# A hybrid mixer block on one core: dilated scores of two heads in one run of 64-row matmuls, and a new order of the down products

## The chip, the cores and the metric

The kernel runs on one core of a Trainium2 chip. The time is that of the device in microseconds (us). The kernel before took 1464.97 us in the median of three runs (1462.9 to 1469.22).

## The reference

A transformer block with a sequence of 1024 and a width of 1024. Four mixers of width 256 (dilated attention, retention, gated linear attention, a state space layer) share one input projection. Then come an output product, a layer norm, an attention to a memory of 256 rows, a second norm, a SwiGLU network of width 2816, and a third norm:

```python
proj = x @ w_in
y = concat(dilated(dq, dk, dv), retention(...), gla(...), s5(...)) @ w_mix_out
x = layer_norm(ALPHA * x + y);  x = layer_norm(ALPHA * x + memory(x, mem))
x = layer_norm(ALPHA * x + (silu(x @ w_gate) * (x @ w_up)) @ w_down)
# dilated: 4 heads of 64; three branches (window 128, 512, 2048; step 1, 4, 16), joined by their softmax sums
s = q @ k.T * 64 ** -0.5 + alibi;  p = exp(s - max);  o = sum over branches of p @ v, over the sum of p
```

## The kernel before, in words

All data is float32. Where one pass is too coarse, a number is split into a high part (rounded to fp32r) and the rest (fp32r too), and a product is high by high, high by low and low by high: `mm3`, three matmuls into one PSUM bank.

**The order.** Every matmul and transpose goes through `mm` or `tp`, and `pin` ties each to the one before: TensorE runs exactly the order in which the code is written. VectorE (DVE), ScalarE (ACT), GpSimd (POOL) and the DMA queue on SyncE (SP) get their order from the framework's scheduler. The mixers are generators. A `yield t` in one lets `weave` (line 106) put projection work between its parts: about t us of it, in steps that the projection declares (0.65 us for three matmuls of 512 columns, tile `fm`); what was given too much is taken off the next yield.

**Dilated attention** (`dilated(f)`, line 962, once for each pair of heads). The three branches become one softmax, with a table `Z` that holds position terms, masks and the log of how many branches see a key. For query block i (128 queries) n = 128 (i+1) keys count. `scores(j)`, j = 2i + h, handles one head: for each 512 keys one matmul with 128 contraction rows (64 rows of the head's high q above 64 rows of its low q, against the high k stacked twice) and one with 64 rows (high q by low k). Then DVE adds `Z` and takes the maximum in one instruction (line 988), negates it (line 990), and ACT takes the exponential in place (line 991). `turn(j)` transposes the result on TensorE into the PSUM tile that held the scores and copies it to `dpT`; `values(i)` multiplies by v, the two heads side by side in 64 columns each. The layout of the stacked operands is made as the projection is evicted: `ev_q` (line 885) with two casts and two subtractions of 64 rows for each half, `ev_k` (line 896) with four casts and two subtractions.

**The last stage** (`ffn`, line 741). The network runs as a Strassen-like scheme of 7 products. Each of the products of the down projection sums over 11 pairs of operands that lie in device memory; `down_raw` loads a pair (two transfers of 256 KB into one of three buffers `wraw`), `versions` splits it on ACT (line 147) and DVE (line 148) into one of four pairs `whi`, `wlo`. `product` runs 12 matmuls for each pair into four PSUM banks and evicts these at its end. The seventh product (A22 by T4) is loaded and split early, a pair at a time, by `keep`, into tiles of its own; the tuple `ahead` says at which steps of a product. `low` evicts and normalises the rows of the first four tiles, `high` those of the last four.

Of the kernel before, what the change touches and what calls it, by code (L numbers as in the profile page):

```python
# [18 lines left out]
P = 128  # L19
# [16 lines left out]
class Kernel:  # L36
# [704 lines left out]
    def ffn(self, out):  # L741
# [25 lines left out]
        for t in range(NT):  # L767
            self.X.append(self.big("X"))
            nc.sync.dma_start(self.X[t], self.xdr[t])
        g, b = self.bcast_row("ln_ff_g"), self.bcast_row("ln_ff_b")  # L770
        self.vs = self.down_stream([("A11", "B11"), ("S2", "T2"), ("A12", "B21"), ("S1", "T1"), ("S4", "B22"),
# [113 lines left out]
    def ev_q(self, name):  # L885
        t = [None, None]
        self.t[name] = t

        def evac(hf, ps):
            if hf == 0:  # L890
                t[:] = [self.big("q", F32R) for _ in range(2)]
            sl, r = slice(hf * 512, (hf + 1) * 512), [slice(0, 64), slice(64, 128)]
            self.split_all([[t[h][r[h], sl], t[h][r[1 - h], sl], ps[r[h]]] for h in range(2)])
        return evac

    def ev_k(self, name):
        res = [None, None, None]
        self.t[name] = res

        def evac(hf, ps):  # L900
            if hf == 0:
                for h in range(3):
                    res[h] = self.big("k", F32R)
            sl = slice(hf * 512, (hf + 1) * 512)
            r = [slice(0, 64), slice(64, 128)]
            for h in range(2):
                self.nc.scalar.copy(out=res[h][r[1 - h], sl], in_=ps[r[h]])
            self.split_all([[res[h][r[h], sl], res[2][r[h], sl], ps[r[h]]] for h in range(2)])
        return evac
# [52 lines left out]
    def dilated(self, f):  # L962
# [8 lines left out]
        pb, tb = [self.big("dp") for _ in range(2)], [self.big("dpT") for _ in range(3)]  # L971
# [3 lines left out]
        def scores(j):  # L975
            i, h = j // 2, j % 2
            n = (i + 1) * P
            if h == 0:
                l[i] = self.small("dl", [P, 2])
            s = st[j] = self.two("ds")  # L980
# [5 lines left out]
            p = pb[j % 2]  # L986
            m = self.small("dm", [P, 1])
            nc.vector.tensor_tensor_reduce(out=p[:, :n], in0=s[:, :n], in1=Z[h][:, 1024 - n:],
                                           scale=0.125, scalar=-3e38, op0=ALU.add, op1=ALU.max, accum_out=m)
            nc.vector.tensor_scalar(out=m, in0=m, scalar1=-1.0, scalar2=None, op0=ALU.mult)  # L990
            nc.scalar.activation(out=p[:, :n], in_=p[:, :n], func=AF.Exp, bias=m, scale=1.0,
                                 accum_out=l[i][:, h:h + 1])

        def turn(j):
            i = j // 2
            p, pT, t = pb[j % 2], tb[j % 3], st.pop(j)
            for b in range(i + 1):
                self.tp(t[:, b * P:(b + 1) * P], p[:, b * P:(b + 1) * P])
            n = (i + 1) * P
            for c0 in range(0, n, 512):  # L1000
                c1 = min(n, c0 + 512)
                self.copy(pT[:, c0:c1], t[:, c0:c1])

        def values(i):
            if i % 4 == 0:
                o[i // 4], rl[i // 4] = self.tr("do"), self.half("drl")
            for b in range(i + 1):
                for h in range(2):
                    hh = 2 * f + h
                    self.mm(o[i // 4][64 * h:64 * h + 64, i % 4, :], v[b][:, hh * 64:(hh + 1) * 64],  # L1010
                            tb[(2 * i + h) % 3][:, b * P:(b + 1) * P], start=b == 0, stop=b == i, tile_position=(0, 64 * h))
# [673 lines left out]
    def items_all(self):  # L1685
# [4 lines left out]
        for f in range(2):  # L1690
            self.item(f"q{f}", self.fill_fm([self.ev_q(f"q{f}")]), fm(2 * f))
            self.item(f"k{f}", self.fill_fm([self.ev_k(f"k{f}")]), fm(2 * f + 1))
# [124 lines left out]
```

## Time and profile before

| | |
|---|---|
| median of the runs | 1464.97 us |
| profiled execution | 1460.22 us, span 1458.4 us |
| TensorE busy | 1420.3 us, 97% of the span |
| VectorE, ScalarE, GpSimd busy | 935.3, 527.3, 329.5 us |
| granted TensorE clock | 0.996 |
| DMA | 193.61 MB, mean 133 GB/s |

The span counts from the first to the last instruction that was profiled. Matmuls are pipelined: one starts before the one ahead of it has ended, so that the time of a run of matmuls is read from start to start, and the share of busy time counts stretches in which the array takes in less than it could. The idle time in front of an instruction is put down to what released it.

### The profile page before, as it was taken

What the parts mean: (1) busy time and instruction counts of PE and PEld (TensorE: products, weight loads), DVE (VectorE), ACT (ScalarE), POOL (GpSimd) and SP (SyncE); (2) the same over time, 40 slices, a digit from 0 to 9 for tenths busy, and PEclk for the clock granted to TensorE, in tenths of its full rate; (3) what the DMA queues carried; (4) which work ended last, traced back from release to release, by engine and by line L of the source; (5) the groups of instructions that cost most, each with busy time, mean ns of one, the idle gap of its engine ahead of it and who ended that gap; (6) DMA issues with size and microseconds to landing.
All of it is one profiled execution on the core that took longest, in us unless ns stands there. A gap on an engine that the chain in (4) does not pass through costs nothing.

```text
span 1458.4 us, 20809 instructions
## 1 busy us (share of the span) xinstructions
PE 1420.3 (97%) x7754; PEld 1160.0 (80%) x7754; DVE 935.3 (64%) x1640; ACT 527.3 (36%) x834; POOL 329.5 (23%) x592
## 2 busy tenths in 40 slices
PE   8998999999999999999999999999999999999987
PEld 6876787788788788888888877788888888888776
DVE  7877545485567379558557987666655555545586
ACT  4224523342245133334344622222222222345452
POOL 2000000010000000000000256767666665000013
PEclk9999999999999999999999999999999999999999
DMA  7431020100438202214312435445545459666752
GB/s 255 131 119 71 30 73 30 43 31 2 151 102 303 88 29 87 73 44 154 107 45 89 156 124 168 164 166 168 183 150 169 170 174 339 200 189 216 230 189 101
DMA packets 76404, 193.61 MB, mean 133 GB/s; under 512 B 9088, under 2 KB 9872, under 8 KB 76304
## 3 DMA queue, kind: packets, MB, share of 16 engines
q1 hardware_dynamic: 74576, 189.15, 39.2%
q10 hardware_dynamic: 1728, 3.15, 0.7%
q8 instruction: 61, 1.00, 0.3%
q14 instruction: 39, 0.32, 0.1%
HBM read 147.04 MB, written 45.22 MB: 132 GB/s over the span
## 4 chain that ended last, share of the span: by engine, by line
PE 78%; DVE 7%; DMA 6%; issue 3%; POOL 3%; ACT 2%; SPq 1%; DVEq 0%; ACTq 0%; POOLq 0%
PE ga L71 9%; PE gc L71 8%; PE fm L71 8%; PE q L71 6%; PE gb L71 6%; PE wo L71 6%; PE mx L71 5%; PE da L71 5%; DVE wlo L148 2%; PE dn L71 2%; PE ds L71 2%; DMA wraw<-tT 2%; PE dr L71 2%; PE p L71 2%; PE gv L71 2%
## 5 line engine op out<-in xcount | busy, mean ns | idle before, releaser
L148 DVE TENSOR_TENSOR wlo<-wraw,whi 128x1024 fp32r<-128x1024 f32 (+3 forms) x180 | 228.3, 1270 | 118.1 <-ACT whi L147 117.2
L147 ACT CAST whi<-wraw 128x1024 fp32r<-128x1024 f32 (+3 forms) x180 | 186.5, 1038 | 309.9 <-PE mx L71 42.1
L71 PE MATMUL ga<-xv,whi 128*128 128x512 f32 x528 | 163.5, 390 | 4.7 <-DVE gq L693 3.5
L71 PEld LDWEIGHTS ga<-xv,whi 128*128 128x128 f32 x528 | 98.7, 188 | 27.8 <-issue 6.9
L71 PE MATMUL gc<-xv,whi 128*128 128x512 f32 x352 | 109.0, 391 | 1.4 <-ACT ge L678 1.4
L71 PE MATMUL gb<-xv,whi 128*128 128x512 f32 x352 | 108.3, 389 | 0.0
L71 PE MATMUL ga<-xv,wlo 128*128 128x512 f32 x264 | 102.7, 389 | 0.0
L71 PE MATMUL fm<-xh,whi 128*128 128x512 f32 x208 | 85.7, 412 | 0.0
L71 PE MATMUL wo<-whi,oT 128*128 128x512 f32 x256 | 82.1, 394 | 0.0
L71 PE MATMUL fm<-xh,wlo 128*128 128x512 f32 x208 | 81.5, 392 | 0.0
L71 PE MATMUL fm<-xl,whi 128*128 128x512 f32 x208 | 81.3, 391 | 0.0
L71 PE MATMUL mx<-whi,yT 128*128 128x512 f32 x256 | 80.6, 392 | 0.6 <-DVE X L352 0.6
L71 PEld LDWEIGHTS gc<-xv,whi 128*128 128x128 f32 x352 | 65.6, 188 | 15.9 <-ACT ge L678 2.3
L71 PEld LDWEIGHTS gb<-xv,whi 128*128 128x128 f32 x352 | 66.1, 188 | 13.7
L71 PE MATMUL gc<-xv,wlo 128*128 128x512 f32 x176 | 68.5, 389 | 0.0
L71 PE MATMUL gb<-xv,wlo 128*128 128x512 f32 x176 | 68.5, 389 | 0.0
L260 POOL TENSOR_TENSOR X<-X,ln_ff_b 128x1024 f32<-128x1024 f32 x7 | 17.7, 2547 | 196.2 <-ACT X L259 196.2
L71 PEld LDWEIGHTS ga<-xv,wlo 128*128 128x128 f32 x264 | 49.6, 188 | 10.3
L71 PEld LDWEIGHTS mx<-whi,yT 128*128 128x128 f32 x256 | 48.1, 188 | 11.3 <-DVE X L352 1.0
L71 PEld LDWEIGHTS wo<-whi,oT 128*128 128x128 f32 x256 | 48.1, 188 | 9.7
L71 PE MATMUL da<-wlo,whi 128*128 128x512 f32 x132 | 51.7, 392 | 3.9 <-DVE wlo L148 3.9
L71 PE MATMUL dr<-whi 128*128 128x512 f32 x132 | 51.6, 391 | 1.7 <-DVE X L781 1.7
(501 smaller groups left out, 3345.8 us busy)
## 6 DMA issues: line engine op xcount, KB each, us to landing
wraw<-in_w_gu SPq DMA_DIRECT2D x28, 512.0 KB, 4.1
gr<-in_w_gu SPq DMA_DIRECT2D x22, 512.0 KB, 4.5
dw<-in_w_down SPq DMA_DIRECT2D x22, 512.0 KB, 3.9
tT<-dw SPq DMA_DIRECT2D x44, 256.0 KB, 2.0
wraw<-hS SPq DMA_DIRECT2D x44, 256.0 KB, 2.9
wraw<-tT SPq DMA_DIRECT2D x44, 256.0 KB, 3.4
wraw<-hA SPq DMA_DIRECT2D x33, 256.0 KB, 2.8
wraw<-in_w_down SPq DMA_DIRECT2D x33, 256.0 KB, 3.0
```

The costliest lines, as they stand in the source:

```text
L71: return self.pin(self.nc.tensor.matmul(*a, **k))
L147: return (self.nc.scalar.copy(out=hi, in_=src), self.nc.vector.tensor_tensor(out=lo, in0=src, in1=hi.bitcast(F32), op=ALU.subtract))
L148: self.nc.vector.tensor_tensor(out=lo, in0=src, in1=hi.bitcast(F32), op=ALU.subtract))
L260: nc.gpsimd.tensor_tensor(out=x, in0=x, in1=b, op=ALU.add)
```

## The change

The scores of both heads are computed by `scores(i)`, in matmuls of 64 contraction rows only, alternating between the heads (rows 0 to 63 and 64 to 127, two PSUM tiles). The stacked operands go, and with them two tiles and the extra casts: `ev_hl` makes one high and one low tile of all 128 rows. The loop turns both heads one behind the other, and the yields are new. In the last stage the products stand in another order, the keeps sit in the third to fifth product, and the loads of x are written in two places.

```diff
-        for t in range(NT):
-            self.X.append(self.big("X"))
-            nc.sync.dma_start(self.X[t], self.xdr[t])
+        def more_x(ts):
+            for t in ts:
+                self.X.append(self.big("X"))
+                nc.sync.dma_start(self.X[t], self.xdr[t])
+
+        more_x(range(4))
...
-        self.vs = self.down_stream([("A11", "B11"), ("S2", "T2"), ("A12", "B21"), ("S1", "T1"), ("S4", "B22"),
+        self.vs = self.down_stream([("A12", "B21"), ("A11", "B11"), ("S2", "T2"), ("S1", "T1"), ("S4", "B22"),
                                     ("S3", "T3")])
...
-        ac = [self.bank("da") for _ in range(4)]
-        product(ac, True, lambda j, ps: add(X[j], hs[0], ps, ALPHA))
-        product(ac, False, lambda j, ps: add(X[j], hs[1], ps, ALPHA))
+        r, ac = [[self.bank(n) for _ in range(4)] for n in ("dr", "da")]
+        product(r, True, lambda j, ps: add(X[j], hs[0], ps, ALPHA))
+        product(ac, True, lambda j, ps: self.residual(X[j], hs[0], 0, ps, 1.0))
+        more_x(range(4, 8))
+        product(ac, False, lambda j, ps: add(X[j], hs[1], ps, ALPHA), (1, 4, 7, 10))
         r = [self.bank("dr") for _ in range(4)]
-        product(r, True, lambda j, ps: self.residual(X[j], hs[0], 0, ps, 1.0))
-        r = [self.bank("dr") for _ in range(4)]
-        product(r, True, lambda j, ps: add(X[4 + j], hs[1], ps, ALPHA), (2, 5, 8))
-        product(r, False, low, (1, 4, 7, 10))
-        product(ac, False, high, (2, 5, 8, 10))
+        product(r, True, lambda j, ps: add(X[4 + j], hs[1], ps, ALPHA), (1, 4, 7, 10))
+        product(r, False, low, (2, 5, 8))
+        product(ac, False, high)
...
+    def ev_hl(self, name):
+        t = []
         self.t[name] = t
 
         def evac(hf, ps):
             if hf == 0:
+                t.extend(self.big(name[0], F32R) for _ in range(2))
             sl = slice(hf * 512, (hf + 1) * 512)
+            self.split_all([[t[0][:, sl], t[1][:, sl], ps]])
         return evac
...
+        def scores(i):
+            n, qt = (i + 1) * P, slice(i * P, (i + 1) * P)
+            l[i] = self.small("dl", [P, 2])
+            for h in range(2):
+                st[2 * i + h] = self.two("ds")
             for c0 in range(0, n, 512):
                 c1 = min(n, c0 + 512)
-                r, qt = slice(64 * h, 64 * h + 64), slice(i * P, (i + 1) * P)
-                self.mm(s[:, c0:c1], q[h][:, qt], k[h][:, c0:c1], start=True, stop=False)
-                self.mm(s[:, c0:c1], q[h][r, qt], k[2][r, c0:c1], start=False, stop=True)
...
+                for a, b in ((0, 0), (1, 0), (0, 1)):
+                    for h in range(2):
+                        r = slice(64 * h, 64 * h + 64)
+                        self.mm(st[2 * i + h][:, c0:c1], q[a][r, qt], k[b][r, c0:c1], start=a + b == 0, stop=b == 1)
+            for h in range(2):
+                s, p = st[2 * i + h], pb[h]
+                m = self.small("dm", [P, 1])
...
         scores(0)
-        scores(1)
         yield 4.45
-        for j in range(17):
-            if j < 16:
-                turn(j)
-            if j and j % 2 == 0:
-                values(j // 2 - 1)
-            if j == 8 or j == 16:
-                back(j // 8 - 1)
-            yield 1.9
-            if j + 2 < 16:
-                scores(j + 2)
+        for i in range(8):
+            turn(2 * i)
+            turn(2 * i + 1)
+            yield 1.3 + 0.1 * i
+            values(i)
+            if i % 4 == 3:
+                back(i // 4)
+            if i < 7:
+                scores(i + 1)
+                yield 1.8 + 0.25 * i
```

Three places show how the instructions move. First TensorE, the scores of query block 4 of the first pair of heads (640 keys). Before, head 0 alone; `ds` is the PSUM tile of a head's scores, `k` and `q` the stacked operands, the transposes (`ident`) are of the block ahead, and `fm` is projection work:

```order
L71 MATMUL fm215_1772<-xl27_314,whi139_1174 128x512
L71 MATMUL fm215_1772<-xh38_360,wlo140_1175 128x512
L71 MATMUL ds219_1806<-k163_1491,q147_1250 128x512
L71 MATMUL ds219_1806<-k165_1495,q147_1250 128x512
L71 MATMUL ds219_1806<-k163_1491,q147_1250 128x128
L71 MATMUL ds219_1806<-k165_1495,q147_1250 128x128
L74 MATMUL ds216_1776<-ident23_267,dp176_1568 128x128 x4
L71 MATMUL fm215_1772<-xh41_390,whi139_1174 128x512
```

The same block now, both heads (`ds218`, `ds219`), `k163` and `q147` the high, `k164` and `q148` the low tiles:

```order
L71 MATMUL ds218_1805<-k163_1487,q147_1250 128x512
L71 MATMUL ds219_1806<-k163_1487,q147_1250 128x512
L71 MATMUL ds218_1805<-k163_1487,q148_1252 128x512
L71 MATMUL ds219_1806<-k163_1487,q148_1252 128x512
L71 MATMUL ds218_1805<-k164_1489,q147_1250 128x512
L71 MATMUL ds219_1806<-k164_1489,q147_1250 128x512
L71 MATMUL ds218_1805<-k163_1487,q147_1250 128x128
L71 MATMUL ds219_1806<-k163_1487,q147_1250 128x128
L71 MATMUL ds218_1805<-k163_1487,q148_1252 128x128
L71 MATMUL ds219_1806<-k163_1487,q148_1252 128x128
L71 MATMUL ds218_1805<-k164_1489,q147_1250 128x128
L71 MATMUL ds219_1806<-k164_1489,q147_1250 128x128
```

Two times four matmuls in two places, of 128 and 64 rows in turn, have become twelve of 64 rows in one run.

Second DVE, query block 7 of the first pair (1024 keys): line 988 (now 977) adds the table and takes the maximum (`dm`, its second row reads that out), line 990 (now 979) negates it for the exponential. Before:

```order
L988 ISA dp_1566,dm_2026<-ds_2021,Z_1560 128x1024
L988 ISA dm_2026 128x1
L184 COPY dpT_1572<-ds_1979 128x512
L990 TENSOR_SCALAR dm_2026<-dm_2026 128x1
L184 COPY gk_1969<-fm_1972 128x512
L988 ISA dp_1568,dm_2054<-ds_2049,Z_1563 128x1024
L988 ISA dm_2054 128x1
L148 TENSOR_TENSOR wlo_2087<-wraw_2084,whi_2086 128x1024
L990 TENSOR_SCALAR dm_2054<-dm_2054 128x1
```

And now:

```order
L977 ISA dp_1552,dm_2056<-ds_2042,Z_1546 128x1024
L977 ISA dm_2056 128x1
L977 ISA dp_1554,dm_2060<-ds_2043,Z_1549 128x1024
L977 ISA dm_2060 128x1
L184 COPY gk_1982<-fm_1985 128x512
L979 TENSOR_SCALAR dm_2056<-dm_2056 128x1
L148 TENSOR_TENSOR wlo_2071<-wraw_2068,whi_2070 128x1024
L979 TENSOR_SCALAR dm_2060<-dm_2060 128x1
```

The negation of the first head, on which its exponential waits, now stands behind the maximum of the second head; a copy or a weight split stands between, as before.

Third SP, the queue where the down products begin: `X` are the loads of x, `wraw` those of the first product's operands, `tT` and `hA` stores of the products before, `ln_ff` the last norm's vectors. Before (four loads of X stand further ahead):

```order
L769 DMA X_10756<-xdr_87 128x1024
L769 DMA X_10759<-xdr_88 128x1024
L609 DMA tT_210<-dw_10730 128x512
L712 DMA hA_161<-h_10482 128x512
L769 DMA X_10762<-xdr_89 128x1024
L609 DMA tT_209<-dw_10732 128x512
L769 DMA X_10765<-xdr_90 128x1024
L217 DMA ln_ff_g_10768<-in_ln_ff_g 128x1024
L609 DMA tT_211<-dw_10732 128x512
L217 DMA ln_ff_b_10771<-in_ln_ff_b 128x1024
L733 DMA wraw_10792<-in_w_down 128x512
L730 DMA wraw_10811<-hA_112 128x512
```

Now (again with four loads of X further ahead):

```order
L217 DMA ln_ff_g_10772<-in_ln_ff_g 128x1024
L217 DMA ln_ff_b_10775<-in_ln_ff_b 128x1024
L609 DMA tT_210<-dw_10746 128x512
L712 DMA hA_161<-h_10498 128x512
L733 DMA wraw_10800<-in_w_down 128x512
L609 DMA tT_209<-dw_10748 128x512
L770 DMA X_11230<-xdr_87 128x1024
L770 DMA X_11233<-xdr_88 128x1024
L609 DMA tT_211<-dw_10748 128x512
L770 DMA X_11236<-xdr_89 128x1024
L770 DMA X_11239<-xdr_90 128x1024
L730 DMA wraw_10819<-hA_113 128x512
```

The later four loads of X are written behind two products, but the scheduler has put them in front of the first product's next pair; what moved is the order among X, the vectors and half a pair.

## Rows read from the trace of the kernel before

**Rows 1.** The page, busy time, share of the span and instructions of each engine:

```profile
PE 1420.3 (97%) x7754; PEld 1160.0 (80%) x7754; DVE 935.3 (64%) x1640; ACT 527.3 (36%) x834; POOL 329.5 (23%) x592
```

**Rows 2.** The page, chain that ended last, by engine:

```profile
PE 78%; DVE 7%; DMA 6%; issue 3%; POOL 3%; ACT 2%; SPq 1%; DVEq 0%; ACTq 0%; POOLq 0%
```

**Rows 3.** Busy time by stretch: both dilated halves, the last product's begin:

```profile
core 0: us, PE busy (x) PEld busy (x) DVE busy (x) ACT busy (x) POOL busy (x), PEclk, DMA share, GB/s
121.00:200.00 79.00, 77.88 (x399) 54.28 (x399) 43.63 (x103) 37.95 (x73) 1.28 (x14) 1.00 0.14 47
200.00:290.00 90.00, 90.00 (x640) 71.01 (x636) 41.50 (x116) 28.35 (x58) 1.77 (x20) 1.00 0.13 42
...
1380.00:1420.00 40.00, 36.11 (x157) 28.95 (x156) 33.04 (x85) 21.87 (x27) 2.76 (x2) 1.00 0.62 193
```

**Rows 4.** Groups of 121 to 290 us, scores: count, busy us, mean ns, idle before:

```profile
L71 PE MATMUL ds<-k,q 128*128 128x512 f32 (+3 forms) x96 | 35.0, 412 | 1.1 <-ACT s5t L1605 1.0
...
L71 PEld LDWEIGHTS ds<-k,q 128*128 128x128 f32 x96 | 17.8, 185 | 18.5 <-issue 14.4 <-ACT s5t L1605 1.2 <-DVE dpT L184 0.5
```

**Rows 5.** Timeline of TensorE, query blocks 3 and 4: start, length, count:

```profile
160.09 0.88 PE L71 MATMUL do<-dpT,dv 128*64 128x128 f32 x12
160.89 0.50 PE L71 MATMUL fm<-xh,whi 128*128 128x512 f32 x1
161.23 0.39 PE L71 MATMUL fm<-xl,whi 128*128 128x512 f32 x1
161.46 0.40 PE L71 MATMUL fm<-xh,wlo 128*128 128x512 f32 x1
...
163.07 1.33 PE L71 MATMUL ds<-k,q 128*128 128x512 f32 x4
164.32 0.66 PE L74 MATMUL ds<-ident,dp 128*128 128x128 f32 x4
```

**Rows 6.** Timeline of TensorE and its weight loads, one score block of retention:

```profile
408.70 0.52 PEld L71 LDWEIGHTS rs<-rq,rk 64*128 64x128 f32 x8 [0.35 <-issue]
408.70 0.72 PE L71 MATMUL rs<-rq,rk 64*128 64x128 f32 x8
...
409.35 0.39 PE L71 MATMUL kt<-memh,whi 128*128 128x256 f32 x1
```

**Rows 7.** Instructions of tile dp: ns least, median, most:

```profile
L988 DVE CUSTOM_DVE_ANT_0 dp<-ds,Z x32: 291/758/1224, 133.9 to 274.3; 128x128 f32<-128x128 f32 x4, 128x256 f32<-128x256 f32 x4, 128x384 f32<-128x384 f32 x4, 128x512 f32<-128x512 f32 x4
L991 ACT ACTIVATE dp<-dp,dm x32: 393/779/1155, 134.6 to 276.6; 128x128 f32<-128x128 f32 x4, 128x256 f32<-128x256 f32 x4, 128x384 f32<-128x384 f32 x4, 128x512 f32<-128x512 f32 x4
```

**Rows 8.** Groups of 121 to 290 us on VectorE and ScalarE:

```profile
L148 DVE TENSOR_TENSOR wlo<-wraw,whi 128x1024 fp32r<-128x1024 f32 x8 | 9.8, 1219 | 0.9 <-ACT whi L147 0.9
...
L154 DVE TENSOR_TENSOR k<-fm,k 64x512 fp32r<-64x512 f32 x8 | 5.5, 687 | 1.6 <-ACT k L152 1.5
L990 DVE TENSOR_SCALAR dm<-dm 128x1 f32<-128x1 f32 x32 | 4.8, 149 | 0.5
L907 ACT CAST k<-fm 64x512 fp32r<-64x512 f32 x8 | 4.6, 581 | 3.5 <-PE fm L71 3.4
...
L988 DVE DVE_READ_ACCUMULATOR2_ANT dm<- 128x1 f32 x32 | 2.7, 83 | 0.0
```

**Rows 9.** The page, down products, first matmuls of the steps: idle before, releaser:

```profile
L71 PE MATMUL da<-wlo,whi 128*128 128x512 f32 x132 | 51.7, 392 | 3.9 <-DVE wlo L148 3.9
L71 PE MATMUL dr<-whi 128*128 128x512 f32 x132 | 51.6, 391 | 1.7 <-DVE X L781 1.7
```

**Rows 10.** Chain of 1331 to 1339 us: one load of the stream, start, us:

```profile
1331.68 4.40 DMA wraw<-tT
...
1336.15 1.06 ACT dv L147
...
1337.30 1.24 DVE dv L148
1338.55 0.32 SPq L730
```

More of the change, by code (lines that the diff above doesn't have):

```diff
@@ L883, in proj_first @@
         self.nc.sync.dma_start(self.ydr[8], t)
-    def ev_q(self, name):
-        t = [None, None]
+    def ev_hl(self, name):
+        t = []
         self.t[name] = t
@@ L890, in evac @@
             if hf == 0:
[L891 to L903, printed above, removed]
+                t.extend(self.big(name[0], F32R) for _ in range(2))
             sl = slice(hf * 512, (hf + 1) * 512)
[L905 to L908, printed above, removed]
+            self.split_all([[t[0][:, sl], t[1][:, sl], ps]])
         return evac
@@ L970, in dilated @@
             Z.append(z)
-        pb, tb = [self.big("dp") for _ in range(2)], [self.big("dpT") for _ in range(3)]
+        pb, tb = [self.big("dp") for _ in range(2)], [self.big("dpT") for _ in range(2)]
         y = self.big("ya")
         st, l, o, rl = {}, {}, {}, {}
[L975 to L980, printed above, removed]
+        def scores(i):
[3 more added lines that the diff above has]
+                st[2 * i + h] = self.two("ds")
@@ L981, in scores @@
             for c0 in range(0, n, 512):
                 c1 = min(n, c0 + 512)
-                r, qt = slice(64 * h, 64 * h + 64), slice(i * P, (i + 1) * P)
-                self.mm(s[:, c0:c1], q[h][:, qt], k[h][:, c0:c1], start=True, stop=False)
-                self.mm(s[:, c0:c1], q[h][r, qt], k[2][r, c0:c1], start=False, stop=True)
[L986 to L989, printed above, removed]
@@ L990, in scores @@
-            nc.vector.tensor_scalar(out=m, in0=m, scalar1=-1.0, scalar2=None, op0=ALU.mult)
-            nc.scalar.activation(out=p[:, :n], in_=p[:, :n], func=AF.Exp, bias=m, scale=1.0,
-                                 accum_out=l[i][:, h:h + 1])
+                for a, b in ((0, 0), (1, 0), (0, 1)):
+                    for h in range(2):
+                        r = slice(64 * h, 64 * h + 64)
+                        self.mm(st[2 * i + h][:, c0:c1], q[a][r, qt], k[b][r, c0:c1], start=a + b == 0, stop=b == 1)
@@ new lines, in scores @@
+            for h in range(2):
+                s, p = st[2 * i + h], pb[h]
+                m = self.small("dm", [P, 1])
+                nc.vector.tensor_tensor_reduce(out=p[:, :n], in0=s[:, :n], in1=Z[h][:, 1024 - n:],
+                                               scale=0.125, scalar=-3e38, op0=ALU.add, op1=ALU.max, accum_out=m)
+                nc.vector.tensor_scalar(out=m, in0=m, scalar1=-1.0, scalar2=None, op0=ALU.mult)
+                nc.scalar.activation(out=p[:, :n], in_=p[:, :n], func=AF.Exp, bias=m, scale=1.0,
+                                     accum_out=l[i][:, h:h + 1])
@@ L994, in turn @@
         def turn(j):
             i = j // 2
-            p, pT, t = pb[j % 2], tb[j % 3], st.pop(j)
+            p, pT, t = pb[j % 2], tb[j % 2], st.pop(j)
             for b in range(i + 1):
@@ L1010, in values @@
                     self.mm(o[i // 4][64 * h:64 * h + 64, i % 4, :], v[b][:, hh * 64:(hh + 1) * 64],
-                            tb[(2 * i + h) % 3][:, b * P:(b + 1) * P], start=b == 0, stop=b == i, tile_position=(0, 64 * h))
+                            tb[h][:, b * P:(b + 1) * P], start=b == 0, stop=b == i, tile_position=(0, 64 * h))
             nc.vector.reciprocal(out=l[i], in_=l[i])
@@ L1690, in items_all @@
         for f in range(2):
-            self.item(f"q{f}", self.fill_fm([self.ev_q(f"q{f}")]), fm(2 * f))
-            self.item(f"k{f}", self.fill_fm([self.ev_k(f"k{f}")]), fm(2 * f + 1))
+            self.item(f"q{f}", self.fill_fm([self.ev_hl(f"q{f}")]), fm(2 * f))
+            self.item(f"k{f}", self.fill_fm([self.ev_hl(f"k{f}")]), fm(2 * f + 1))
         self.item("gk", self.fill_fm([self.ev_fm("gk", 0)]), fm(12))
```

## Prediction

> **What bounds the kernel.** I read the page's busy times first: TensorE has work in flight for 97% of the span [rows 1]; then the chain that ended last: 78% of it is TensorE [rows 2]. So time is won only where TensorE needs less of it or waits less, and the next view is the busy time by stretch. The two dilated halves lie between 121 and 290 us, and there TensorE is busy for 77.9 of 79 us and all of 90 us [rows 3]; its one wait at the scores is 1.0 us at the start [rows 4]. VectorE and ScalarE are half idle there. What the change saves on TensorE in these halves is therefore saved in full, and any wait it brings in is paid in full, since TensorE keeps the written order. At the end of the program the down products wait: 3.9 us for a weight split and 1.7 us for an eviction [rows 9], 5.6 us together.
>
> **Scores, what goes.** 96 matmuls keep TensorE busy for 35.0 us [rows 4]. A block's end overlaps the next start: the block at 163.07 lasts 1.33 us, the transposes begin at 164.32, 0.08 us before its end [rows 5]. For some 30 blocks that is 2.4 us, so the scores take 32.6 us from start to start. The block of 1.25 us has four matmuls, two of 512 and two of 128 columns. A plain 512-column matmul follows the one ahead by 0.23 us (161.23 to 161.46) [rows 5], so the four would take some 0.7 us; the rest is the change between 128 and 64 rows, four times in the block.
>
> **Scores, what comes.** 144 matmuls of 64 rows, that is 72 steps of two heads. Whether the two of a step run together is not shown by the old scores, which never put the two halves of the rows side by side. The nearest row is retention's score block, where heads alternate between the same two halves of rows: eight matmuls of 128 columns last 0.72 us, and the next product starts 0.65 us after the first of them [rows 6]. Four 128-row transposes of 128 columns take 0.66 us [rows 5], so twice as many half-row matmuls take the same: they go two by two. That block gives four steps of about 0.11 us and 0.2 us for changing into and out of 64 rows. A projection matmul behind such a change takes 0.34 us instead of 0.23 (160.89 to 161.23 to 161.46) [rows 5], 0.1 us more.
>
> The blocks of 128 to 1024 keys make, for both halves, 36 steps of 512 columns and 12 each of 128, 256 and 384. By 0.23 us for 512, 0.11 for 128, and 0.12 and 0.17 for those between (interpolated), that is 8.3 + 1.3 + 1.4 + 2.0 = 13.0 us. Sixteen runs with 0.3 us of changes add 5.0: 18.0 us. Twelve value runs that went back to projection work now lead into the scores, and their 0.1 us each goes too, 1.3 us with rounding. So 32.6 + 1.3 - 18.0 = 16 us are won. Bounds: 21 us if changes cost nothing, 3 us if the two of a step do not overlap at all (13 us more).
>
> A row of the trace decides on the weight loads too: in retention's block eight loads lie within 0.52 us, beside matmuls that last until 0.72 us [rows 6], so loads for a half of the rows do not wait until that half's matmul is through. The Trainium skill says otherwise (page "TensorE: Matmul & The Clock Gate", section "The mechanism"): a weight load overlaps matmuls in flight only when its row group differs. By that rule the second and third pair of weights of each run would be exposed, and the score runs would come out near the unpaired bound; the trace speaks against it.
>
> **Scores, the wait that comes in.** Before, the next head's scores, other transposes and projection work always lay between a head's scores and its transposes. Now both heads are scored together and only a yield of 1.8 to 3.3 us stands before both are turned. The maximum takes 0.29 us for 128 keys up to 1.22 for 1024, the exponential 0.39 to 1.16 [rows 7], a negation 0.15 and the read-out 0.08 [rows 8]. VectorE's new order runs both maxima before the first negation. So the first head is ready 2 maxima + 1 exponential + 0.4 us (read-outs, negation, hand-over) after the scores, the second one exponential and 0.1 us later. Weave's carrying over gives 3, 3, 3, 4, 5, 5, 5 groups of three projection matmuls (0.69 us each) for blocks 1 to 7: 2.1, 2.1, 2.1, 2.8, 3.5, 3.5, 3.5 us. Block 3 (512 keys): ready after 2 x 0.69 + 0.73 + 0.4 = 2.5 us, 0.4 late; the second head after 3.3, when 0.44 us of transposes have moved TensorE to 2.9: 0.4 late again. Block 7: 4.0 and 5.3 us against 3.5 and 4.9: 0.9 late. All seven: 0, 0.4, 0.8, 0.5, 0.1, 0.5, 0.9 = 3.2 us, twice 6.4. A copy or a weight split (1.22 us [rows 8]) in front of a negation adds to a few of them: I take 7 us. Below, the bound is 0 (projection work of gv covers more than I count); above, 6.4 + 14 x 1.22 = 23 us, a split in front of every turn. Behind each waiting transpose stand the values, the next scores and the projection work: all of TensorE.
>
> **Edits that cost nothing.** The evictions lose 16 casts of 0.58 us on ScalarE and 8 subtractions of 0.69 us on VectorE [rows 8]. They lie beside a full TensorE; without that cover they would be worth some 9 us. Two tiles fewer, and 1.2 us less projection work asked for in each half, move work to later parts and change no sum. The loads of X stay in front of the first product by SP's order; were they to push its operands back, it would be one load, 4.4 us [rows 10].
>
> **Down products.** A load takes 4.40 us, its cast 1.06, its subtraction 1.24, the next issue 0.32 [rows 10]: 7.0 us in three buffers, 2.34 us a load. TensorE takes a pair every 12 x 0.23 = 2.75 us. A product without keeps gains 4.5 us on TensorE, one with four keeps (15 loads, 35.1 us against 30.3) loses 4.8. Both versions put 11 keeps into three neighbouring products: 25.7 us of loads against 13.5 us of spare time, 12.2 us behind. Waits of 5.6 us show, so what is loaded and split ahead covered 6.6. The new order moves this forward. At the fourth product's end eight keeps have gone through instead of three: 8 x 2.34 - 22 x 0.41 = 9.7 us behind, 3.1 more than that cover, beside the 1.7 us of that eviction, which sits behind splits in VectorE's queue. The fifth loses about 1 more. The last product is freed of four keeps, but the norms still fill VectorE (33 of 40 us [rows 3]), so of 3.9 us there I keep 1.7. Sum 7.5 against 5.6: 2 us lost. Bounds: 5.6 us won, 6.6 lost.
>
> **Sum.** -16 + 7 + 2 = -7 us on the profiled execution's 1460.22 us: 1453. The median of the runs is 1464.97, 4.8 above it, so I predict 1458 for the median; all times below are on that footing.
>
> **Rivals.** (A) The new waits stay under 3 us and the keeps save 2: -16 + 3 - 2 = -15, 1450. For it: VectorE is busy for only 44 of 79 us [rows 3]. Against: the order of the negations.
> (B) The steps do not overlap, in the streams or in the weight loads: 13 us more, -3 + 7 + 2 = +6, 1471. For it: the mean load of the scores' weights is 0.185 us [rows 4], and 64-row matmuls of this type and 512 columns side by side are in no row. Against: [rows 6]. The Trainium skill's rule above would bring it about by the loads.
> (C) Slower: the transposes wait for VectorE at every turn, because a split or copy of the projection sits between maximum and negation. Place: line 979. Price: 23 us of waits, -16 + 23 + 2 = +9, 1474. It decides from 14 us of waits on; slower beyond 0.5% from 21. For it: such a split stands there at block 7, and ScalarE already depends on these negations. Against: the splits are only 8 in both halves [rows 8].
> (D) The stream loses its full 6.6 us: -16 + 7 + 7 = -2, 1463. For it: three products with keeps follow each other as before. The part of the change that should spread the loads of X does not do it by SP's order, in every case.
>
> **Chances.** Forecast 0.45 (its own range 1452 to 1464), A 0.20, B 0.12, C 0.12, D 0.11. What a measurement of this kernel can tell from no change is 0.5%, 7.3 us. Faster than that: A, and half of the forecast, 0.43. Slower: most of C and a third of B, 0.15. Within: 0.42. The range 1446 to 1474 leaves out the best end of A and the far end of C.
>
> **What would show it.** Right: the scores' busy time falls from 35.0 to about 20 us, two `ds` matmuls start within some 0.02 us of each other, and the transposes `ds<-ident,dp` show 5 to 10 us of idle time behind the exponential (line 980 then). B would show score blocks of four or six matmuls that follow each other by 0.23 us. C would show over 14 us at the transposes. In the down products I expect the wait at the fourth product's end to grow to 4 or 5 us and those of the last to shrink. The prediction is wrong if the score runs take over 25 us, if the transposes wait for nothing, or if the down products' waits vanish.

## The result, and the profile after

In the first comparison the changed kernel takes 1444.26 us (median of 4 runs, 1443.01 to 1448.66) against 1463.93 (1460.83 to 1469.22): ratio 0.987, 95% interval 0.985 to 0.989. In a second one (a_again below) it is 1443.22 against 1462.23, 0.986 (0.985 to 0.988). That is 19 to 20 us faster, where 7 were forecast.

The first page of the changed kernel, busy times and the chain by engine, against [rows 1, 2]: TensorE is busy for 15 us less, with 48 matmuls more.

```profile
PE 1405.3 (97%) x7802; PEld 1155.9 (80%) x7802; DVE 916.7 (64%) x1632; ACT 518.7 (36%) x818; POOL 330.6 (23%) x588
```
```profile
PE 80%; DVE 9%; DMA 5%; issue 2%; ACT 2%; POOL 1%; SPq 1%; DVEq 0%; ACTq 0%; POOLq 0%
```

Groups of 121 to 292 us after, scores and transposes (count, busy us, mean ns, idle before), against [rows 4]:

```profile
L74 PE MATMUL ds<-ident,dp 128*128 128x128 f32 x144 | 21.1, 280 | 4.5 <-ACT dp L980 3.8
L71 PE MATMUL ds<-k,q 64*128 64x512 f32 (+3 forms) x144 | 17.6, 363 | 1.1 <-ACT s5t L1593 1.1
...
L71 PEld LDWEIGHTS ds<-k,q 64*128 64x128 f32 x144 | 11.9, 185 | 5.8 <-issue 2.4 <-ACT s5t L1593 1.2 <-POOL k L134 0.8
```

The scores fall from 35.0 to 17.6 us of busy time; from start to start, added up over all blocks without the 1.1 us wait inside the first one, from 33.0 to 16.5. The transposes, which never waited, now wait 4.5 us, 3.8 of them for the exponential. The timeline of TensorE around the 896-key block of the first half (start, length, count) answers [rows 5]: twelve score matmuls from 174.44 until the projection at 175.85, 1.41 us.

```profile
172.97 1.53 PE L71 MATMUL do<-dpT,dv 128*64 128x128 f32 x24
174.44 1.49 PE L71 MATMUL ds<-k,q 64*128 64x512 f32 x12
175.85 0.50 PE L71 MATMUL fm<-xh,whi 128*128 128x512 f32 x1
176.19 0.39 PE L71 MATMUL fm<-xl,whi 128*128 128x512 f32 x1
```

One such wait, on VectorE: the 1024-key block of the first half. Both maxima, a copy, and only then the negation (189.72); behind it a weight split before the second one (190.91). The transposes start at 191.25, 1.06 us late.

```profile
186.82 1.23 DVE L977 CUSTOM_DVE_ANT_0 dp<-ds,Z 128x1024 f32<-128x1024 f32 x1 [4.66 <-PE ds L71]
...
187.97 1.22 DVE L977 CUSTOM_DVE_ANT_0 dp<-ds,Z 128x1024 f32<-128x1024 f32 x1
...
189.11 0.69 DVE L184 COPY gk<-fm 128x512 f32<-128x512 f32 x1
189.72 0.14 DVE L979 TENSOR_SCALAR dm<-dm 128x1 f32<-128x1 f32 x1
189.78 1.21 DVE L148 TENSOR_TENSOR wlo<-wraw,whi 128x1024 fp32r<-128x1024 f32 x1
190.91 0.14 DVE L979 TENSOR_SCALAR dm<-dm 128x1 f32<-128x1 f32 x1
```

The down products, against [rows 9, 10]: the waits of the last product (3.9 us) and the 1.7 us are gone, and one of 4.4 has come. The group from the page, then the chain that leads to it:

```profile
L71 PE MATMUL dr<-whi 128*128 128x512 f32 x132 | 52.5, 397 | 4.4 <-DVE X L784 4.4
```
```profile
1332.36 3.99 DMA wraw<-tT
1336.36 0.02 issue
1336.38 1.05 ACT dv L147
...
1337.51 0.42 DVE dv L148
1337.93 0.72 issue
1338.65 0.69 DVE X L784
1339.34 0.14 issue
1339.48 1.62 PE dr L71 x3
```

The fourth product's first eviction stands on VectorE behind the split of a kept operand whose load landed at 1336.36. The fifth product writes the same banks and waits until 1339.48. While TensorE waits its granted clock falls to 0.50, the 1.2 GHz level, and stays there for some 4 us of work (stretches of 2 us: busy PE, PEld, DVE, ACT, POOL, PEclk, DMA share, GB/s):

```profile
1334.00:1336.00 2.00, 1.11 (x5) 0.57 (x4) 1.03 (x1) 0.94 (x1) 0.00 (x0) 1.00 0.75 259
...
1338.00:1340.00 2.00, 0.52 (x1) 0.50 (x2) 2.00 (x3) 0.99 (x1) 0.00 (x0) 0.50 0.77 235
...
1342.00:1344.00 2.00, 2.00 (x6) 1.52 (x6) 1.40 (x2) 0.00 (x0) 0.00 (x0) 0.50 0.77 285
1344.00:1346.00 2.00, 2.00 (x11) 1.62 (x10) 0.51 (x1) 1.65 (x2) 0.00 (x0) 1.00 0.79 236
```

**Where the time went.** Four profiles of each kernel were taken in the end (before, b_again, b_c, b_d; after, a_again, a_c, a_d). Each is cut by the starts of the same matmuls: the last `sv` of the state space layer (S5), the last `rs` (retention's scores), the first and the last `dr`/`da` (the down products' banks). Times in us:

| stage | before | after | mean difference |
|---|---|---|---|
| start to last `sv` | 94.5, 94.6, 92.7, 96.2 | 92.0, 94.0, 92.7, 95.3 | -1.0 |
| last `sv` to last `rs` (S5's end, dilated halves) | 346.2, 346.2, 347.6, 349.2 | 331.5, 331.6, 331.5, 332.5 | -15.5 |
| last `rs` to first down product | 791.7, 795.9, 791.2, 793.1 | 791.7, 789.8, 793.3, 790.2 | -1.7 |
| down products | 186.4, 185.7, 186.0, 186.2 | 186.6, 186.3, 187.4, 187.8 | +1.0 |
| span | 1458.4, 1462.0, 1457.1, 1464.4 | 1441.4, 1441.3, 1444.6, 1445.4 | -17.3 |

Only the second row stands clear of its own spread. Part of it lies ahead of the dilated halves, where the prediction had not looked. The stretch from the last `sv` to the last `glu` (S5's closing product), in before and after (columns as above):

```profile
94.45:132.85 38.40, 34.82 (x377) 25.02 (x376) 32.78 (x55) 15.29 (x23) 1.25 (x16) 1.00 0.19 59
```
```profile
91.95:126.55 34.60, 34.60 (x377) 25.06 (x375) 31.59 (x54) 10.34 (x15) 1.56 (x17) 1.00 0.21 69
```

The same 377 matmuls take 3.8 us less: before, TensorE was idle for 3.6 of them while VectorE was busy for 32.8 of 38.4. The groups of S5's outputs (`s5z` is the tile of its states) and of q's evictions say what for (before, then after):

```profile
L71 PE MATMUL sy<-s5z,s5C 128*32 128x128 f32 x256 | 7.6, 274 | 3.6 <-DVE s5z L1530 3.6
...
L154 DVE TENSOR_TENSOR q<-fm,q 64x512 fp32r<-64x512 f32 x4 | 2.8, 688 | 0.1
```
```profile
L71 PE MATMUL sy<-s5z,s5C 128*32 128x128 f32 x256 | 7.4, 273 | 0.0
...
L154 DVE TENSOR_TENSOR q<-fm,q 128x512 fp32r<-128x512 f32 x2 | 1.4, 687 | 0.8 <-POOL q L134 0.8
```

Before, all four subtractions of q stand between S5's first products with `sv` and its last shift of `s5z`; that chain takes 18.0 us on VectorE, and 12.7 after. The subtractions are 2.8 of these 5.3 us; for the rest, the last shift now goes ahead of a weight split and of steps behind `sy`.

### The profile page after: what moved, and what is told of

It is laid out like the page before. It is cut to its first block, busy times and chain, and to the rows that moved or that the text cites. A ratio compares the mean times of both kernels' runs of the same rounds, so it can differ in the third digit from the quotient of the medians.

```text
span 1441.4 us, 20876 instructions
## 1 busy us (share of the span) xinstructions
PE 1405.3 (97%) x7802; PEld 1155.9 (80%) x7802; DVE 916.7 (64%) x1632; ACT 518.7 (36%) x818; POOL 330.6 (23%) x588
## 4 chain that ended last, share of the span: by engine, by line
PE 80%; DVE 9%; DMA 5%; issue 2%; ACT 2%; POOL 1%; SPq 1%; DVEq 0%; ACTq 0%; POOLq 0%
PE ga L71 10%; PE fm L71 7%; PE gb L71 7%; PE gc L71 7%; PE da L71 6%; PE q L71 6%; PE dr L71 6%; PE wo L71 6%; PE mx L71 5%; PE dn L71 2%; PE s L71 2%; DVE wlo L148 2%; PE pv L71 2%; PE rv L71 2%; PE gv L71 1%
## 5 line engine op out<-in xcount | busy, mean ns | idle before, releaser
L147 ACT CAST whi<-wraw 128x1024 fp32r<-128x1024 f32 (+3 forms) x180 | 186.6, 1038 | 306.8 <-PE mx L71 42.2
L71 PE MATMUL dr<-whi,wlo 128*128 128x512 f32 x132 | 52.1, 395 | 0.0
```

Source lines behind the costliest of these rows:

```text
L71: return self.pin(self.nc.tensor.matmul(*a, **k))
L147: return (self.nc.scalar.copy(out=hi, in_=src), self.nc.vector.tensor_tensor(out=lo, in0=src, in1=hi.bitcast(F32), op=ALU.subtract))
```

## The experiments

**What the evictions are worth (e1, e11).** e1 splits q and k by halves again (the edit below); e11 does so for the operands of the first dilated half alone.

```diff
-            self.split_all([[t[0][:, sl], t[1][:, sl], ps]])
+            r = [slice(0, 64), slice(64, 128)]
+            if name[0] == "k":
+                if hf == 0:
+                    t.append(self.big("k", F32R))
+                for h in range(2):
+                    self.nc.scalar.copy(out=t[2][r[h], sl], in_=ps[r[h]])
+            self.split_all([[t[0][r[h], sl], t[1][r[h], sl], ps[r[h]]] for h in range(2)])
```

> The changed kernel with the evictions of q and k made in halves of 64 rows again (two casts and two subtractions where the change makes one of each, and two more casts of k into a spare tile, as before); scores and down products as changed. Theory: the 3.58 us in which TensorE waited for s5z at 116.04 us in the kernel before went because VectorE has half as many subtractions of q to do in the S5 stage. Then that wait comes back with 2 to 4 us, VectorE needs some 17 us again from the first product of s5z with sv to the last shift of s5z (17.3 before, 12.0 in the changed kernel), and the time is 1447 to 1450 us against 1444.26. Rival: the wait went because TensorE's granted clock did not fall to 0.50 behind the transfer waits at 88 to 91 us, as it did in the profiled run of before; then there is no wait over 0.5 us at that place and the time is 1443 to 1446.

> The changed kernel with the evictions of q and k of the first dilated half alone made in halves of 64 rows again (with the spare copy of k); those of the second half whole. Theory: what the halves cost in the S5 stage comes from the first half's evictions alone, and what they cost in the dilated stretch from the second half's, which stand on ScalarE and VectorE among the maxima. Then the piece from the last sv to the last glu matmul takes 38.5 to 39.2 us (34.6 changed, 39.0 with all halves) and from the first to the last score 129.6. Rival: the later end of S5 shifts loads and splits among the maxima: 38.5 to 39.2 and 132 to 133 us.

e1: 1454.08 us (ratio 0.994, 0.992 to 0.996), more than either theory said. Its waits in S5 come to 3.7 us, spread over two places, where 2 to 4 at one were expected (groups of e1):

```profile
L71 PE MATMUL sy<-s5z,s5C 128*32 128x128 f32 x256 | 7.6, 274 | 1.1 <-DVE s5z L1524 1.1
...
L71 PE MATMUL glu<-su,w_glu 128*128 128x512 f32 x16 | 7.6, 605 | 2.6 <-DVE su L1583 2.6
```

The chain to the last shift takes 13.8 us, not the 17 expected: VectorE takes its work in another order, and the debt shows at `su` instead. From the last `sv` to the last `glu` it is 39.0 us (34.6 changed, 38.4 before: with the old evictions nothing is gained there), from the first to the last score 132.9 (129.6 changed), the transposes wait 6.8 us. In e11 the same two are 39.0 and 129.6: the first half's evictions cost 4.4 us in S5, the second half's 3.3 among the maxima. The new waits there, 0.5 us at 143.32 and 1.6 at 177.16, follow evictions at 139 to 142 and 170 to 173 us. From the last `sv` to the last `rs` e1 takes 339.25 us: of the 14.7 us between the undisturbed 346.2 and 331.5, 7.7 are the evictions and 7.0 all the rest. The rival (a fall of the clock alone) is out: e1's granted clock is 1.00 throughout this stretch. By the medians e1 gains 8.6 us on its chip and the changed kernel 19 to 20 on others, 10 to 11 us for the evictions; the two intervals leave room for 7.7, and no run shows more of them than that.

**Are the two heads side by side? (e2, e6)** e2 writes head 0's three terms and then head 1's; e6 keeps the written order, but reads both heads from rows 0 to 63 (head 1's own scores are left out). The first edit below is e2's, the second e6's.

```diff
-                for a, b in ((0, 0), (1, 0), (0, 1)):
-                    for h in range(2):
+                for h in range(2):
+                    for a, b in ((0, 0), (1, 0), (0, 1)):
...
-                        r = slice(64 * h, 64 * h + 64)
+                        r = slice(0, 64)
```

> The changed kernel with the loop over the heads put outside the loop over the three terms of a score block: three matmuls of 64 rows of head 0, then three of head 1, on the same tiles. Theory: the gain of the scores is the two heads side by side. Then the 72 steps of two take twice as long; 13 us more on TensorE in the two halves, the starts of neighbouring score matmuls lie 0.2 us apart at 512 columns instead of some 0.01, and since the first head is complete earlier, up to 4.5 us of the waits at the transposes go: 1453 to 1457 us. Rival: 64-row matmuls do not overlap, and the gain is from fewer changes between 128 and 64 rows alone: within 2 us of 1444.26.

> The changed kernel with both heads' scores read from rows 0 to 63, so that head 1 gets head 0's scores (its part of the output is left out in this sense); number, sizes and written order of the matmuls as changed. Theory: the two heads run side by side because they use different halves of the rows, in whatever order they are written. With one half the 144 matmuls follow each other and take twice as long: 29 to 30 us from start to start instead of 16.5, 139 to 143 us from the first to the last score, neighbours of 512 columns 0.23 us apart. Rival: a matmul of 64 rows takes half the time by itself: 16.5 us again.

The 896-key block's timeline in e2, then in e6:

```profile
177.31 1.50 PE L71 MATMUL ds<-k,q 64*128 64x512 f32 x12
178.73 0.50 PE L71 MATMUL fm<-xh,whi 128*128 128x512 f32 x1
```
```profile
179.56 2.71 PE L71 MATMUL ds<-k,q 64*128 64x512 f32 x12
182.20 0.50 PE L71 MATMUL fm<-xh,whi 128*128 128x512 f32 x1
```

In e6 the block takes 2.64 us instead of 1.41, all scores 29.5 us from start to start instead of 16.5: the heads do run side by side, and 13.0 us hang on it, as forecast. In e2 the block takes 1.42 us, all scores 16.8: my theory of e2 fell. The matmuls still start in pairs 10 ns apart, though each run of three on one half is written ahead of the other half's, and stands so in the built program; in e6, with both on one half, 512-column neighbours start 0.23 us apart. So TensorE starts a matmul for the other half of the rows ahead of earlier ones. That the e2 kernel takes 1447.0 us (0.990, 0.988 to 0.992) does not come from the scores: from the first to the last one it takes 128.5 us, 1.1 less than the changed kernel. The Trainium skill (page "TensorE: Matmul & The Clock Gate", section "Part 3: Packing small matmuls — row/col tiling") says that matmuls in distinct row groups run at the same time; both runs agree.

**What the transposes wait for (e5, e9).** e5 puts the second maximum behind the first negation on VectorE; e9 leaves VectorE's order and negates on ScalarE, with the read-outs kept behind the second exponential. Of e5's edit the new edge (`w` is the maximum, `neg` the negation of head 0), of e9's the negation:

```diff
+                if h:
+                    self.order(w, neg)
...
-                nc.vector.tensor_scalar(out=m, in0=m, scalar1=-1.0, scalar2=None, op0=ALU.mult)
...
+                nc.scalar.mul(out=m, in_=m, mul=-1.0)
```

> The changed kernel with one edge more: VectorE's maximum of the second head comes after the negation of the first one's. Theory: the first head's exponential waits for the second head's maximum because of VectorE's order, 0.29 to 1.22 us a block. Then of the 4.5 us in which TensorE waits at the transposes of the two halves 1.5 to 2.5 are left, and from the first to the last score it takes 127 to 127.7 us instead of 129.6. Rival: what the transposes wait for is something else in front of the maximum or the exponential (a weight's split or cast, or that the exponential of the second head has to follow the first): 4 to 5 us of waits again, 129.6 us.

> The changed kernel with the negation of the maximum made on ScalarE, right in front of the exponential that needs it, and a block's read-outs of transposes on ScalarE kept behind the second exponential. Theory: the waits at the transposes come from VectorE's order alone: the second maximum, or a weight's split, between a maximum and its negation. Without a negation on VectorE neither can hold an exponential up: the waits at the transposes fall from 4.5 us to under 1.5, and from the first to the last score it takes 124.5 to 126 us instead of 129.6. Rival: the chain of maximum and exponential is itself too long for what lies between scores and transposes: 3 us of waits or more, 128 us or more.

The transposes' group in e5, then in e9:

```profile
L74 PE MATMUL ds<-ident,dp 128*128 128x128 f32 x144 | 20.0, 276 | 5.1 <-ACT dp L982 5.1
```
```profile
L74 PE MATMUL ds<-ident,dp 128*128 128x128 f32 x144 | 19.9, 276 | 3.5 <-ACT dp L980 3.2
```

Both theories fall short. In e5 no first head waits any more, but the second does: at 1024 keys a weight split now stands between the second maximum and its negation, and the wait is 1.8 us. First to last score 128.4 us. In e9 it is 126.8, 2.8 us less than changed, but the idle time at the transposes falls by 1.0 only. Most of the rest is that transposes and projection matmuls follow each other more closely (15.2 to 14.1 and 74.9 to 74.2 us from start to start). The 3.5 us that are left are mostly not the rival, the chain of maximum and exponential itself: ScalarE puts other work between the two heads. Its timeline in e9 at the first half's 384-key block, where the second head's transposes are 1.15 us late:

```profile
146.33 0.62 ACT L980 ACTIVATE dp<-dp,dm 128x384 f32<-128x384 f32 x1
...
147.04 1.03 ACT L147 CAST whi<-wraw 128x1024 fp32r<-128x1024 f32 x1
147.97 0.57 ACT L152 CAST q<-fm 128x512 fp32r<-128x512 f32 x1
148.45 0.61 ACT L980 ACTIVATE dp<-dp,dm 128x384 f32<-128x384 f32 x1
```

A weight's cast stands there too at the wait of 1.09 us at 251.48, a copy of some 0.6 us at those of 0.40 (240.82) and 0.31 (262.61); these four are 2.95 of the 3.5 us. In the changed kernel such a cast stands ahead of the late exponential at 145.48 (0.94 us) and, beside VectorE's order, at 249.69 (1.27). What the chain costs without them no run shows. (One run each, 1449.86 and 1445.63 us.)

**The down products (e3, e4, e7, e8, e10).** e3 has the old order; e4 spreads the kept operands; e7 swaps the third and fourth product, so that neighbours never share banks; e8 is both; e10 is e8 with e9. Of the edits, the first two products in e4 and e8, then the swap in e7 (the stream of loads is swapped likewise):

```diff
-        product(r, True, lambda j, ps: add(X[j], hs[0], ps, ALPHA))
-        product(ac, True, lambda j, ps: self.residual(X[j], hs[0], 0, ps, 1.0))
+        product(r, True, lambda j, ps: add(X[j], hs[0], ps, ALPHA), (5, 8))
+        product(ac, True, lambda j, ps: self.residual(X[j], hs[0], 0, ps, 1.0), (2, 5, 8))
```

```diff
-        product(ac, False, lambda j, ps: add(X[j], hs[1], ps, ALPHA), (1, 4, 7, 10))
         r = [self.bank("dr") for _ in range(4)]
         product(r, True, lambda j, ps: add(X[4 + j], hs[1], ps, ALPHA), (1, 4, 7, 10))
+        product(ac, False, lambda j, ps: add(X[j], hs[1], ps, ALPHA), (1, 4, 7, 10))
```

> The changed kernel with the down products, their kept operands and the loads of X as before the change; scores and evictions as changed. Theory: the new order of the down products is worth about nothing (186.7 us from the first matmul to the last before, 186.9 after): waits of 5.6 us instead of 4.4, but no fall of the granted clock behind them as at 1337.6 to 1344 us of the changed kernel: 1441 to 1446 us, with the last product's waits of some 3.9 us back and the wait at the fourth product's end gone. Rival: the reordering is a gain of its own that the profiled runs hide: 1447 to 1451 us.

> The changed kernel with the eleven kept operands loaded in the first five products, two or three in each and none in a product's last two steps, instead of four, four and three in the third to the fifth. Theory: the 4.37 us wait at the fourth product's end (its first eviction sits on VectorE behind the subtraction of a kept operand whose load landed late) is a debt of the stream, and the clock of 0.50 behind it costs some 2 us more. Then no wait over 1 us is left in the down products, the clock stays at 1.00 there, and the time is 1437 to 1440 us. Rival: the stream of loads is the limit over all six products, and the wait only moves: waits of 3 to 5 us in sum elsewhere in the down products, 1443 to 1446 us.

> The changed kernel with the third and the fourth down product in the other order, so that the two sets of four banks take turns (r, ac, r, ac, r, ac) and no product's first matmuls need banks that the product just ahead of it has filled; kept operands in the third to the fifth product as changed. Theory: the 4.37 us wait is the eviction of the fourth product, late behind a kept operand's subtraction, in front of a fifth product in the same banks. Then it goes, the weight splits come in time, the clock does not fall there, and the six products take 180 to 183 us instead of 186.6: 1438 to 1441 us. Rival: the stream's debt is behind it: the wait turns up as waits of 3 to 5 us for wlo or whi in the fourth to sixth product: 185 to 188 us, no gain.

> The alternating order of the six down products with the eleven kept operands spread over the first five of them, two or three in each. Theory: with alternating banks no eviction holds a product up, and what is left (3.5 us of waits for wlo in the fourth to sixth product) is the debt of eleven kept operands in three products; spread over five, the spare time of each (some 4.5 us) pays for its own two. Then the waits in the down products are under 1 us in sum and the six products take 182 to 183.5 us from first to last start instead of 185.2: 1438 to 1442 us. Rival: the loads of X ahead of the first and the third product use up the same spare time, and waits of 2 to 4 us for splits stay: 185 us, 1443 to 1446.

> The changed kernel with the negation on ScalarE, the read-outs behind the second exponential, the alternating order of the down products and the kept operands spread over five products. By the theories of the two parts some 4 us are won in the dilated halves and 3 to 4 in the down products: 1435 to 1439 us. By the rivals 1442 to 1446.

| | median us, ratio to before | products us | waits in them |
|---|---|---|---|
| e3 | 1442.87, 0.988 (0.985 to 0.990) | 186.1 | 1.1 eviction, 2.8 split |
| e4 | 1446.04, 0.989 (0.987 to 0.991) | 188.9 | 3.9 + 2.1 eviction |
| e7 | 1444.43, 0.987 (0.985 to 0.990) | 185.2 | 3.5 split, 0.3 cast |
| e8 | 1443.86, 0.988 (0.985 to 0.991) | 186.8 | 3.7 split and cast |
| e10 | 1441.50, 0.987 (0.984 to 0.989) | 182.6 | 1.9 + 0.2 split |

e3 bears out its theory: the old order is worth as much as the new one. e4 fell: 3.9 us of waits came at the end of the second product, the next pair of neighbours with the same banks, and 2.1 stayed at the fourth's. e7 has no eviction's wait any more and gets 3.5 us of waits for splits; the larger group:

```profile
L71 PE MATMUL da<-wlo,whi 128*128 128x512 f32 x132 | 51.7, 392 | 2.0 <-DVE wlo L148 2.0
```

e8 and e10 have the same down products, and differ by 4.2 us in one profile each: e8's has 1.6 us more of waits and a fall of the granted clock at 1296 to 1299 us that e10's lacks. The intervals of all five overlap. In e7, e8 and e10 all that is left are waits for splits and casts of the stream's loads, and none of these orders is shown to be better. On one chip e10's median is 2.4 us below e8's; the 2.8 us in its dilated halves show in its profile too (126.8), but that it beats the changed kernel (0.987 and 0.986 on other chips) is not shown.

**What the stages leave open (b_again, a_again, b_c, b_d, a_c, a_d): the two kernels again, no edit.**

> The kernel before, once more, for a second profile. Theory: the start of the program (the same instructions in every kernel so far; the first dv matmul at 41.7 to 47.1 us in six profiles) and the transfer waits at 87 to 93 us differ from execution to execution, but the piece from the last sv to the last glu matmul does not: 38.4 us again, 34.6 with the new evictions. And from the first to the last score 140.9 us again, within 0.3. Rival: the wait of 3.58 us for s5z in the first profile is chance as well; then that piece takes some 34.6 us here.

> The changed kernel once more, against the kernel before on one chip in more rounds. Theory: the part of the change is the piece from the last sv matmul to the last of retention's scores, 346.2 us before and 331.5 to 331.6 in the changed kernel, 14.7 us, and the down products add nothing; the further 5 us of the first comparison (19.7 us between the medians) are the spread of the executions (the start, and the falls of TensorE's granted clock). Then the profile shows 331.5 us for that piece again, a start of the dv matmuls between 41.7 and 47.1 us, and the medians differ by 14 to 17.5 us. Rival: the change also has fewer or shorter falls of the clock or a faster start of its own: the medians differ by 18 us or more again.

> The kernel before, a third profile. Theory: the 4 us that the stages leave open are TensorE's granted clock (mean 0.993 over nine runs of before, 0.995 over five of the changed kernel; 0.002 of 1450 us is some 3 us); before loses them behind a wait that the changed kernel hasn't: the 3.6 us wait for s5z at 116 us, behind which the clock stays at 1.00 in two profiles but falls to 0.50 in others. Then one of the two new profiles of before shows such a fall at 116 to 121 us. Rival: the falls lie where both kernels wait (17, 90, 455 to 470, 845 to 930 us and in the down products) and before has more of them in the down products or elsewhere.

> The kernel before, a fourth profile: as for the third one. In every one of them the piece from the last sv matmul to the last of retention's scores takes 346.2 us, if the clock doesn't fall in it.

> The changed kernel, a third profile. Theory: 331.5 us from the last sv matmul to the last of retention's scores; granted clock of 1.00 throughout that piece. Rival: the clock falls in that piece in some executions of this kernel too.

> The changed kernel, a fourth profile. Theory: 331.5 us again from the last sv matmul to the last of retention's scores, at a granted clock of 1.00. Rival: a fall of the clock in that piece.

b_again repeats S5's wait (3.60 us) and the 140.9 us between first and last score: neither was chance. a_again repeats 331.6 us, but its medians differ by 19.0: its theory fell on that number. b_c and b_d then show a part that the first profiles had not: the granted clock falls during the wait for `s5z`, which the changed kernel hasn't. The stretch behind it in b_d, and in the first profile, where the same instructions lie some 1.7 us earlier:

```profile
116.00:118.00 2.00, 0.07 (x4) 0.07 (x8) 1.96 (x4) 0.00 (x0) 0.07 (x1) 0.75 0.68 244
118.00:120.00 2.00, 2.00 (x40) 1.85 (x44) 1.30 (x3) 0.63 (x1) 0.04 (x1) 0.50 0.05 18
120.00:122.00 2.00, 2.00 (x47) 1.84 (x43) 1.16 (x2) 0.00 (x0) 0.00 (x0) 0.50 0.00 0
```
```profile
116.00:118.00 2.00, 1.96 (x72) 1.97 (x76) 1.30 (x3) 0.63 (x1) 0.10 (x1) 1.00 0.12 47
118.00:120.00 2.00, 2.00 (x58) 1.73 (x51) 1.68 (x3) 0.00 (x0) 0.23 (x3) 1.00 0.04 8
```

From the last `sv` to the last `glu` these two take 39.8 and 41.4 us instead of 38.4. Of the changed kernel's profiles none has such a fall; a_d has one at 90 to 97 us, behind waits for transfers (2.6 us at `sv`), which costs 1 us in the table's second row.

## Why the prediction was wrong

- **Scores, -16: right.** 33.0 to 16.5 us from start to start. The forecast's 18.0 (17.8 by its factors, since 16 times 0.3 is 4.8) held 0.1 us on a projection matmul behind each run; counted with these, some 15 us are won, since the projection matmuls between the last `sv` and the last `rs` take 1.6 us more (168.1 to 169.7). The 1.3 us behind the value runs came, but each value run now follows projection work and costs the last matmul of it 0.1 us. Rival B is excluded by e6: without the overlap it is 13.0 us more. Nor did the loads of weights get in the way: pairs of 512 columns follow each other by 0.23 us.
- **Waits at the transposes, +7: right in kind, near in size partly by luck.** 4.5 us of idle time, 6.8 with the old evictions (e1). The cause named, VectorE's order, is only part of it: without a negation on VectorE (e9) the two halves are 2.8 us shorter, but 3.5 us of idle time stay, 2.95 of them behind casts and copies on ScalarE between the two heads, which the sum did not hold. Rival C's split shows at the 1024-key block, but all waits together stay far below its 14 us.
- **Edits that cost nothing, 0: the step that failed.** The prediction priced the lost casts and subtractions at some 9 us if their cover were gone and said that they "lie beside a full TensorE". e1 measures 7.7 us. The cover was missing in both places. The first half's evictions lie inside S5 at 96 to 131 us, those of q (to 115) ahead of the stretch whose windows were read [rows 3], and there TensorE waited 3.6 us for VectorE. The second half's lie among the very maxima whose lateness the step before had priced. An eviction beside a busy TensorE still delays what TensorE waits for next.
- **Down products, +2: near, but partly by luck.** The wait at the fourth product's end is 4.4 us (4 to 5 forecast); the last product's went to zero in the first profile instead of 1.7. So the idle time fell from 5.6 to 4.4 us, where 7.5 were forecast. The fall of the clock behind the new wait, in all four profiles, was not in the sum: it eats what the waits gave. +1.0 over four profiles; with the old order e3 takes 186.1 us.
- **The sum.** From the last `sv` to the last `rs` of the first profiles, the work from start to start: score runs -16.6, projection +1.6, other work +0.7; waits at S5's `s5z` -3.6, at scores and transposes +4.5, elsewhere -1.3: -14.7. Without the evictions it is -7.0 (346.2 to 339.25; -16 + 7 = -9 forecast), and they are the other 7.7. The falls of the clock behind S5's wait, 1.4 and 3.1 us in two of four profiles of before, add to the gain. Profiles give 17.3 us, medians 19 to 20, so some 2 us stay open, within the spread of the first and third stage; no run settles whether they belong to the change. Rival A came nearest (1450), but for other reasons than its own: the waits were not under 3 us, and the new order of the down products saved nothing.

## What to carry to other kernels

Before an edit is priced at nothing, find the stretch in which each of its instructions runs, and read that stretch's wait, not its neighbour's: here the removed work sat on the engine that TensorE waited for. A wait on TensorE costs its length and, in some executions, some us of work at half the clock behind it, so one profile is not enough where a few us matter. When a wait at a bank's reuse is taken away from a stream that is behind, look for the same debt at the next load.

## What was not expected of the hardware

- Matmuls of 64 rows start out of their written order when they use the other half of the rows: 16.8 us for runs of three on one half (e2) against 16.5 interleaved and 29.5 with both heads on one half (e6).
- TensorE's clock falls to 0.50 behind some waits and not behind others of the same length: behind S5's 3.6 us in two of four profiles of before.
